# Two unused fills that shift tile addresses in an expert-choice MoE block, so that both matmul operands start at the same offset modulo 512 bytes

## The chip, the cores and the metric

One Trainium2 chip, one of its cores. The kernel is one program, launched once. The metric is the device time of one execution in microseconds (us); three executions of the kernel before took 1856.73 to 1860.6 us, with a median of 1858.37 us. Another execution was profiled, and all rows below come from it.

## The reference

One transformer block on a sequence of 1024 tokens of width 1024, in float32. What matters here is its second half, a mixture of 16 experts, and the projection ahead of it:

```python
mix = jnp.concatenate([y_mlstm, y_attn], axis=-1) @ w_out[l]
x = x + gate1 * mix
h2 = rms_norm(x, norm2_g[l]) * (1.0 + scale2) + shift2
...
cap = (EC_CAPACITY_FACTOR * S) // N_EXPERTS          # 128 tokens for each expert
gates, idx = lax.top_k(affinity.transpose(0, 2, 1), cap)
xin = h[bidx, idx]
hid = jax.nn.silu(jnp.einsum('becd,edf->becf', xin, w_gate)) * jnp.einsum('becd,edf->becf', xin, w_up)
y = jnp.einsum('becf,efd->becd', hid, w_down) * gates[..., None].astype(h.dtype)
```

Each expert takes 128 tokens through `w_gate` and `w_up` (1024 x 2048) and `w_down` (2048 x 1024). Ahead of that stand the input projection, an mLSTM mixer and a dilated attention.

## The kernel before

**Precision.** Float32 products are made of three products of a shorter type: each operand is split in a high part (rounded to `F32R`) and a low part (the rest), and hi x hi, lo x hi and hi x lo are added up in PSUM. In the names, `wh`/`wl`, `xTh`/`xTl`, `hTh`/`hTl`, `ogh`/`ogl` are such pairs; `hT` of the experts holds both parts in one tile.

**Experts (`phase_experts`).** The weights come in 384 pieces of 1 MB (128 partitions x 2048 floats), 24 for each expert, through a ring of ten buffers and some tiles that are reused for the same purpose. `feed` issues the load of a piece on SP's queue as soon as its buffer is free. `cut` splits a piece: ScalarE copies it into `wh` (line 1489), VectorE subtracts to get `wl` (line 1490). Both have three buffers. `mm` (line 1509) then runs 12 matmuls of 128x128 by 128x512 on it. The weight piece is the moving operand, 512 columns at a time; the stationary operand is a 128x128 slice of the transposed tokens `xTh`, `xTl` (gate and up) or of the transposed hidden values `hT` (down). For gate and up the order is four matmuls with `wh` and `xTh`, four with `wh` and `xTl`, four with `wl` and `xTh`; for down eight with `wh` and `hT` (high and low) and four with `wl` and `hT`. Each matmul has its own weight load (PEld), which runs beside the matmul before it.

So there are 16 x 16 x 12 = 3072 matmuls of the gate and up kind and 16 x 8 x 12 = 1536 of the down kind. Between them TensorE makes small transposes (of `xin`, line 1523, and of `hid`, line 1545, six groups for each expert) and eight small matmuls that pick the next expert's tokens (line 1436).

**Output projection (`mix_stream`, `phase_out`).** Here `ogh`, `ogl`, `mix` and `yal` are stationary and `wmh`, `wml`, `woh`, `wol` moving (lines 1069 to 1071 and 1174 to 1176; 384 matmuls of 512 columns).

**Earlier stages.** In `phase_start`, `gates_proj` and `gate_stream` (lines 337, 339, 341) and in `proj_stream` (lines 398 to 400) the operands are `hTh`/`hTl` and split pieces of `w_in`, also with 512 columns.

**Where tiles lie.** Tiles are given out from pools. Pools lie one behind the other from the low end of a partition, or with `side="right"` from its high end, and what is added in an early pool shifts all later pools of its side. The pool `consts` (`k.cp`, opened first on the low side) holds tiles of 512, 512, 32, 32, 512, 256 and 128 bytes for each partition and starts at address 16512, so what follows on that side (`og`, `ya`, and in their buffers `xTl`, `hT`, `ogl`, `yal`) starts at 64 modulo 512. Byte offsets modulo 512 of the operands, in the built programs:

| stage | stationary | moving | before: stationary / moving | after |
|---|---|---|---|---|
| start and projection (L337-341, L398-400) | `hTh`, `hTl` or split `w_in` | the other | 448 / 448 | 448 / 448 |
| experts, gate and up | `xTh` | `wh`, `wl` | 0 / 0 | 0 / 0 |
| experts, gate and up | `xTl` | `wh` | 64 / 0 | 0 / 0 |
| experts, down | `hT` | `wh`, `wl` | 64 / 0 | 0 / 0 |
| output projection | `ogh`, `mix` | `wm*`, `wo*` | 192 / 192 | 0 / 0 |
| output projection | `ogl`, `yal`, three tiles of four | `wmh`, `woh` | 64 / 192 | 0 / 0 |
| output projection | `ogl`, `yal`, one tile of four | `wmh`, `woh` | 192 / 192 | 0 / 0 |

`xTh`, `wh` and `wl` lie at the high side (addresses from 159232 up), `xTl` and `hT` at the low side (from 18496 and from 34880).

Of the kernel before, what the change touches and what calls it, by code (L numbers as in the profile page):

```python
# [11 lines left out]
F32 = mybir.dt.float32  # L12
# [8 lines left out]
P = 128  # L21
# [77 lines left out]
def interleave(*streams):  # L99

    live = [[0.0, n, g, w] for n, (g, w) in enumerate(streams)]
    while live:
        s = min(live, key=lambda x: (x[0], x[1]))
        try:
            s[0] += next(s[2]) * s[3]
        except StopIteration:
            live.remove(s)


class K:  # L110
# [3 lines left out]
    def pool(self, name, stack, bufs=1, space=None, side=None):  # L114
# [4 lines left out]
            kw["side"] = side  # L119
        return stack.enter_context(self.tc.tile_pool(**kw))  # L120

    def split(self, hi, lo, src):
        self.nc.scalar.activation(hi, src, AF.Copy)  # L123
        self.nc.vector.tensor_sub(lo, src, hi)  # L124
# [16 lines left out]
    def consts(self):  # L141
        nc, I = self.nc, self.I
        cp = self.cp
        self.ident = cp.tile([P, P], F32, name="ident")
        make_identity(nc, self.ident)
        self.ones = cp.tile([P, P], F32, name="ones")
        nc.vector.memset(self.ones, 1.0)
        self.c_sb = cp.tile([P, KT], F32, name="c_sb")
        nc.scalar.dma_start(out=self.c_sb, in_=I["c"].rearrange("o (p k) -> p (o k)", k=KT))
        self.sc = cp.tile([P, KT], F32, name="silu_c")  # L150
        self.w4 = self.tmp.tile([P, 3, MH, 4], F32, name="w4")
        for q, name in enumerate(("w_q_blk", "w_k_blk", "w_v_blk")):
            src = I[name]
            nc.gpsimd.dma_start(out=self.w4[:, q], in_=bass.AP(tensor=src.tensor, offset=src.offset, ap=[[4, P], [4 * P, MH], [1, 4]]))

        self.vec_rows = {}
        self.vcols = cp.tile([P, P], F32, name="vcols")
        self.amat = self.mc.tile([P, MH, P], F32, name="amat")
        self.bdv = self.mc.tile([P, MH, P], F32, name="bdv")
        self.mask = self.mc.tile([P, 2, P], F32, name="mask")  # L160
        self.gbias = self.mc.tile([36, 2], F32, name="gbias")
        self.gqk = cp.tile([P, AE], F32, name="gqk")
        self.modc = cp.tile([P, 4 * KT], F32, name="mod_cols")
        rows = self.tmp.tile([P, P], F32, name="vrows")
        nc.vector.memset(rows, 0.0)
        at = 0
        for name, n in (("b_ada", 48), ("norm1_g", 8), ("conv_w", 20), ("conv_b", 4), ("mlstm_norm_g", 4), ("mlstm_skip", 4), ("norm2_g", 8)):
            src = I[name]
            nc.gpsimd.dma_start(out=rows[at:at + n, :], in_=bass.AP(tensor=src.tensor, offset=src.offset, ap=[[P, n], [1, P]]))
            self.vec_rows[name] = at  # L170
            at += n
        self.vrows = rows
# [12 lines left out]
    def phase_start(self):  # L185
# [6 lines left out]
        with ExitStack() as st:  # L192
# [50 lines left out]
            w_next()  # L243
            consts = self.mlstm_consts()
            next(consts)
            mods = []

# [22 lines left out]
            def modulate(k):  # L270
# [3 lines left out]
                self.split(self.hTh[:, k, :], self.hTl[:, k, :], xT[:, k, :])  # L274

            side = itertools.chain(consts, self.attn_tables())
            ada_half(0)
            ada_load(1, own())
# [865 lines left out]
    def phase_out(self):  # L1144
# [4 lines left out]
        with ExitStack() as st:  # L1149
# [55 lines left out]
            for k in range(MH):  # L1205
                if k == MH - 1:
                    for _ in merge:
                        pass
                prep(k)
                if k == 1:  # L1210
                    for i in range(NT):
                        x_load(i)
                for n in range(2 * G1):
                    mm(pss[n], n // 2, n % 2, k)
                    next(consts, 1)
                    if n % 2:
                        next(merge, 1)
# [406 lines left out]
def body(tc, I, out):  # L1624
    with ExitStack() as ctx:
        k = K(ctx, tc, I, out)
        st_ps = ExitStack()
        k.psA = k.pool("ps_a", st_ps, bufs=4, space=PSUM)
        k.psB = k.pool("ps_b", st_ps, bufs=4, space=PSUM)
        k.cp = k.pool("consts", ctx)  # L1630
        k.st_tmp, k.st_proj, k.st_y, k.st_mp = ExitStack(), ExitStack(), ExitStack(), ExitStack()
        k.mc = k.pool("mlstm_const", k.st_proj, side="right")
        k.tmp = k.pool("tmp", k.st_tmp)
        k.consts()
        k.phase_start()
        k.gates_proj()
        k.qkv_d = tc.dram_tile([3, S, ML], F32, name="qkv_d")
        st_cw = ExitStack()
        k.cw = k.pool("mlstm_work", st_cw, side="right")
        k.tags = dict(W=2, qw=2, kw=2, q=1, v=2, h=1, xc=2)  # L1640
        interleave((k.proj_stream(), 1.0), (k.mlstm_stream(), 1.9), (k.ada_stream(), 1.0))
        st_cw.close()
        k.st_mp.close()
        k.yap = k.pool("ya", k.st_y)
        k.ya = [k.yap.tile([P, S], F32, name="ya", bufs=MH) for i in range(MH)]
        st_r, st_aa = ExitStack(), ExitStack()
        k.aa = k.pool("attn_in", st_aa)
        k.pairs, k.kl = {}, {}
        k.ta = k.pool("attn_t", st_aa)
        k.attn_load_qk(0)  # L1650
        k.attn_load_1(0)
        for n, _ in enumerate(k.gate_stream()):
            if n == PAIR0[0]:
                k.attn_pair_norm(0)
                T = k.attn_pair_T(0, lambda: k.psB.tile([P, 512], F32, name="pb"), k.ta)
            if n == PAIR0[1]:
                k.attn_load_2(0)
            if n >= PAIR0[2]:
                next(T, 0)
        for _ in T:  # L1660
            pass
        k.st_proj.close()
        st_ps.close()
        st_m = ExitStack()
        k.m1 = k.pool("moe1", st_m, side="right")
        k.rp = k.pool("rows", st_r, side="right")
        k.mx = k.pool("mix", st_r, side="right")
        st_at = ExitStack()
        k.phase_attn(st_at)
        st_at.close()  # L1670
        st_aa.close()
        st_rt = ExitStack()
        k.rt = k.pool("route", st_rt)
        st_ps = ExitStack()
        k.psm = k.pool("ps_m", st_ps, bufs=8, space=PSUM)
        st_w = ExitStack()
        k.ring = [k.pool("ring_a", st_w, bufs=EARLY)]
        k.flow, k.fed, k.ready = k.pieces(), [], []
        k.phase_out()
        st_r.close()  # L1680
        k.m2 = k.pool("moe2", st_m, side="right")
        k.ring.append(k.pool("ring_b", st_w, bufs=RING - EARLY))
        k.route_select()
        st_ps.close()
        st_ps = ExitStack()
        k.psx = k.pool("ps_x", st_ps, bufs=4, space=PSUM)
        k.psy = k.pool("ps_y", st_ps, bufs=4, space=PSUM)
        k.phase_experts()
        st_ps.close()
        st_w.close()  # L1690
        st_rt.close()
        k.st_y.close()
        st_m.close()
# [29 lines left out]
```

## Time and profile before

| | |
|---|---|
| median of three runs | 1858.37 us (1856.73 to 1860.6) |
| the profiled execution's own time | 1857.18 us |
| its span, from the first to the last instruction | 1855.5 us |
| mean granted TensorE clock | 0.983 of full speed |
| TensorE (PE) busy | 1738.8 us, 94% |
| VectorE (DVE) busy | 1486.8 us, 80% |
| ScalarE (ACT) busy | 1206.2 us, 65% |
| GpSimd (POOL) busy | 179.6 us, 10% |
| bytes moved by DMA | 517.39 MB, mean 279 GB/s |

The experts take the span from about 720 us on. "Busy" of an engine is the union of its instructions' times. A matmul's own duration contains its run through the array, so matmuls overlap in the records; how fast they follow each other is read from the starts, as the time from one start to the next (the pace).

### The profile page before, as it was taken

How to read it: one execution, taken by the hardware profiler on the slowest of the kernel's cores; microseconds unless marked ns; L12 is line 12 of the kernel's file. 1: busy time of each engine (PE TensorE's matmuls, PEld its weight loads, DVE VectorE, ACT ScalarE, POOL GpSimd, SP SyncE). 2: the span in 40 equal slices, each digit the busy share in tenths (PEclk: the TensorE clock that was granted, in tenths of full speed). 3: DMA queues.
4: the chain of work that ended last, by engine and by line, in shares of the span. 5: the costliest groups of instructions: out<-in, count | busy, mean ns of one | idle time of the engine just before them, and what ended most of it. 6: DMA issues, size and time to landing. Idle time of an engine off the chain costs nothing. (4 is left out here: it accounts for less than half of the span.)

```text
span 1855.5 us, 24345 instructions
## 1 busy us (share of the span) xinstructions
PE 1738.8 (94%) x8685; PEld 1400.1 (75%) x8685; DVE 1486.8 (80%) x2147; ACT 1206.2 (65%) x1596; POOL 179.6 (10%) x176
## 2 busy tenths in 40 slices
PE   5999999999998939999999999999999999999997
PEld 4777788778886727888888777787777777777875
DVE  5578885687865778988988888898888888988976
ACT  5346454477763438777777677777776776777764
POOL 1001000031122010011011000100100001000001
PEclk9999999999999959999999999999999999999999
DMA  8135662435648777999999999999999999999991
GB/s 321 47 108 188 208 209 89 108 89 118 139 112 239 270 306 278 382 356 371 392 351 389 348 347 351 362 367 358 352 343 383 349 354 360 336 377 356 357 357 23
DMA packets 150536, 517.39 MB, mean 279 GB/s; under 512 B 32938, under 2 KB 50736, under 8 KB 112784
## 3 DMA queue, kind: packets, MB, share of 16 engines
q1 hardware_dynamic: 136832, 482.07, 70.6%
q0 software_dynamic: 10528, 33.18, 7.1%
q8 instruction: 68, 1.11, 0.2%
q10 hardware_dynamic: 3056, 0.61, 0.2%
q14 instruction: 52, 0.43, 0.1%
HBM read 488.29 MB, written 27.50 MB: 278 GB/s over the span
## 5 line engine op out<-in xcount | busy, mean ns | idle before, releaser
L1490 DVE TENSOR_TENSOR wl<-w,wh 128x2048 fp32r<-128x2048 f32 x295 | 663.2, 2279 | 72.9 <-ACT wh L1489 72.0
L1489 ACT ACTIVATE wh<-w 128x2048 fp32r<-128x2048 f32 x295 | 557.7, 1914 | 120.2 <-PE px L1509 56.3
L1490 DVE TENSOR_TENSOR wl<-w_half,wh 128x1024 fp32r<-128x1024 f32 x178 | 207.9, 1218 | 8.3 <-ACT wh L1489 8.2
L1489 ACT ACTIVATE wh<-w_half 128x1024 fp32r<-128x1024 f32 x178 | 179.8, 1059 | 36.8 <-PE px L1509 16.3
L1509 PE MATMUL px<-wl,xTh 128*128 128x512 f32 x512 | 142.5, 398 | 10.0 <-DVE wl L1490 10.0
L1509 PE MATMUL py<-wl,xTh 128*128 128x512 f32 x512 | 142.6, 398 | 8.9 <-DVE wl L1490 8.8
L1509 PE MATMUL px<-wh,xTh 128*128 128x512 f32 x512 | 141.9, 397 | 3.5 <-ACT wh L1489 1.9
L1509 PE MATMUL py<-wh,xTh 128*128 128x512 f32 x512 | 142.6, 396 | 0.8 <-ACT wh L1489 0.7
L1509 PE MATMUL px<-wh,xTl 128*128 128x512 f32 x512 | 141.4, 397 | 0.0
L1509 PE MATMUL py<-wh,xTl 128*128 128x512 f32 x512 | 141.1, 395 | 0.0
L1509 PE MATMUL px<-wh,hT 128*128 128x512 f32 x512 | 131.5, 397 | 0.0
L1509 PE MATMUL py<-wh,hT 128*128 128x512 f32 x512 | 130.8, 397 | 0.2 <-ACT wh L1489 0.2
L1509 PEld LDWEIGHTS px<-wl,xTh 128*128 128x128 f32 x512 | 94.8, 189 | 38.7 <-DVE wl L1490 18.1
L1509 PEld LDWEIGHTS py<-wl,xTh 128*128 128x128 f32 x512 | 94.1, 188 | 38.1 <-DVE wl L1490 17.8
L1562 POOL DMA_INDIRECT out_dram<-xin,idx x16 | 52.6, 3288 | 661.2 <-DVE xin L1561 661.2
L1509 PEld LDWEIGHTS px<-wh,xTh 128*128 128x128 f32 x512 | 95.2, 189 | 26.6 <-ACT wh L1489 3.6
L1509 PEld LDWEIGHTS px<-wh,xTl 128*128 128x128 f32 x512 | 96.8, 189 | 21.9
L1509 PEld LDWEIGHTS py<-wh,hT 128*128 128x128 f32 x512 | 95.1, 188 | 23.4 <-ACT wh L1489 0.9
L1509 PEld LDWEIGHTS py<-wh,xTh 128*128 128x128 f32 x512 | 94.4, 188 | 24.2 <-ACT wh L1489 3.1
L1509 PEld LDWEIGHTS py<-wh,xTl 128*128 128x128 f32 x512 | 96.1, 188 | 21.8 <-DVE xTl L124 0.2
L1509 PEld LDWEIGHTS px<-wh,hT 128*128 128x128 f32 x512 | 95.0, 188 | 22.6 <-ACT wh L1489 0.4
L398 PE MATMUL pa<-wh,hTh 128*128 128x512 f32 x192 | 78.9, 412 | 1.6 <-ACT wh L355 1.5
(452 smaller groups left out, 3091.9 us busy)
## 6 DMA issues: line engine op xcount, KB each, us to landing
w<-in_w_gate_dram SPq DMA_DIRECT2D x99, 1024.0 KB, 7.3
w<-in_w_down_dram SPq DMA_DIRECT2D x99, 1024.0 KB, 9.6
w<-in_w_up_dram SPq DMA_DIRECT2D x94, 1024.0 KB, 6.2
w_half<-in_w_up_dram SPq DMA_DIRECT2D x62, 512.0 KB, 7.2
w_half<-in_w_gate_dram SPq DMA_DIRECT2D x56, 512.0 KB, 8.2
w_half<-in_w_down_dram SPq DMA_DIRECT2D x56, 512.0 KB, 8.7
ada_w<-in_w_ada_dram SPq DMA_DIRECT2D x64, 256.0 KB, 3.4
wraw<-in_w_in_dram SPq DMA_DIRECT2D x20, 512.0 KB, 4.5
```

The source lines that it names most:

```text
L398: nc.tensor.matmul(ps, hTh[:, k, t], hi[k], start=(k == 0), stop=False)
L1489: self.nc.scalar.activation(h[:, c], t, AF.Copy)
L1490: self.tc.keep_in_program_order(self.nc.vector.tensor_sub(l[:, c], t, h[:, c]))
L1509: nc.tensor.matmul(ps[c], x[:, t], y[:, o:o + 512], start=first and q == 0 and t == 0, stop=last and (q, t) == (2, FF // N - 1))
L1562: nc.gpsimd.indirect_dma_start(out=self.out, out_offset=bass.IndirectOffsetOnAxis(ap=u["idx"][:, :1], axis=0), in_=y, in_offset=None, comp ...
```

## The change

A helper `fill` allocates a tile that nobody reads, and writes zeros to it on GpSimd. It is called twice: 448 bytes per partition in `consts`, ahead of all other tiles of that pool, and 192 bytes in `rows`, on the high side, ahead of the pools of the output projection. The first shifts everything behind it on the low side up by 448 bytes, the second the pools behind `rows` down by 192 bytes. `consts` is opened for the whole kernel; `rows` is closed before the experts begin.

```diff
@@ -119,6 +119,10 @@
             kw["side"] = side
         return stack.enter_context(self.tc.tile_pool(**kw))
 
+    def fill(self, pool, n):
+
+        self.nc.gpsimd.memset(pool.tile([P, n // 4], F32, name="fill"), 0.0)
+
@@ -141,6 +145,7 @@
         cp = self.cp
+        self.fill(cp, 448)
         self.ident = cp.tile([P, P], F32, name="ident")
@@ -1664,6 +1669,7 @@
         k.rp = k.pool("rows", st_r, side="right")
+        k.fill(k.rp, 192)
         k.mx = k.pool("mix", st_r, side="right")
```

Of the instructions' order it moves little: two writes are added on GpSimd, and one pair of instructions on VectorE changes places. Lines of the changed kernel are 4 to 6 higher. GpSimd's queue at the start of the program, before:

```order
L1715 MEMSET const-uint8-127 128x1
L1719 UNCONDITIONAL_BRANCH
masks.py:197 MEMSET ident 128x128
L154 DMA w_80<-in_w_q_blk_dram 128x4x4
masks.py:199 ISA
```

and now:

```order
L1721 MEMSET const-uint8-127 128x1
L1725 UNCONDITIONAL_BRANCH
L124 MEMSET fill 128x112
masks.py:197 MEMSET ident 128x128
L159 DMA w_82<-in_w_q_blk_dram 128x4x4
masks.py:199 ISA
```

The fill stands ahead of `ident` and of the first small loads. The second fill stands in the same queue in the attention, ahead of two writes to `kTl` (lines 770 before, 775 now), which before follow the products `qk` directly. Now:

```order
L763 TENSOR_TENSOR qk<-qk,gqk 128x1024 x2
L124 MEMSET fill 128x48
L775 MEMSET kTl_3708 64x1024
L775 MEMSET kTl_3710 64x1024
L1059 TENSOR_TENSOR wo_raw<-wo_raw,gate_3433 128x512 x2
```

VectorE's queue in the normalization at the start (`n_v` and `n_y` belong to the second half of `x`, `vcols` are constants that a transpose on TensorE delivers), before:

```order
L453 TENSOR_TENSOR bdv<-bmask,w_80 128x128 x4
L133 TENSOR_SCALAR n_v<-ss_111 128x4
L134 TENSOR_SCALAR n_y<-n_v 128x4
L178 COPY vcols<-pa 128x128
L136 TENSOR_TENSOR n_t<-n_y 128x4
```

and now:

```order
L458 TENSOR_TENSOR bdv<-bmask,w_82 128x128 x4
L137 TENSOR_SCALAR n_v<-ss_113 128x4
L183 COPY vcols<-pa 128x128
L138 TENSOR_SCALAR n_y<-n_v 128x4
L140 TENSOR_TENSOR n_t<-n_y 128x4
```

The copy of `vcols` goes ahead of `n_y`. On TensorE, ScalarE and SP's queue the instructions and their order are the same.

## Rows read from the trace of the kernel before

**Rows 1.** Windows of the experts: length, busy us by engine, clock, DMA share, GB/s.

```profile
760.00:1000.00 240.00, 240.00 (x1101) 195.00 (x1100) 214.56 (x158) 182.79 (x161) 26.23 (x7) 1.00 0.97 375
1000.00:1800.00 800.00, 777.44 (x3486) 616.12 (x3485) 681.51 (x492) 577.40 (x516) 52.89 (x21) 1.00 0.95 357
```

**Rows 2.** Waits of TensorE from 720 us on: total us, times, longest.

```profile
PE px L1509 <- DVE wl L1490: 11.5, 19, 1.4
PE py L1509 <- DVE wl L1490: 9.0, 15, 1.4
```

**Rows 3.** Timeline of TensorE in the start stage: start us, length, instruction, count.

```profile
97.38 0.62 PE L341 MATMUL pa<-hTh,wg_l 128*128 128x512 f32 x2
...
102.82 0.62 PE L341 MATMUL pa<-hTh,wg_l 128*128 128x512 f32 x2
```

**Rows 4.** Timeline of TensorE in a gate product of the experts.

```profile
1197.88 1.08 PE L1509 MATMUL px<-wh,xTh 128*128 128x512 f32 x4
...
1203.43 0.85 PE L1509 MATMUL px<-wh,xTh 128*128 128x512 f32 x3
```

**Rows 5.** Windows as in rows 1, around rows 3 and rows 4.

```profile
97.40:103.80 6.40, 6.40 (x30) 5.31 (x29) 0.00 (x0) 0.00 (x0) 0.00 (x0) 1.00 0.30 80
1195.00:1209.00 14.00, 13.59 (x59) 10.56 (x58) 11.58 (x7) 9.17 (x6) 1.45 (x1) 1.00 0.99 370
```

**Rows 6.** Timeline of TensorE in narrow windows, inside two groups of rows 4.

```profile
1201.12 0.61 PE L1509 MATMUL px<-wh,xTh 128*128 128x512 f32 x2
1201.57 0.40 PE L1509 MATMUL px<-wh,xTl 128*128 128x512 f32 x1
1202.04 0.63 PE L1509 MATMUL px<-wh,xTl 128*128 128x512 f32 x2
```

**Rows 7.** Timeline of TensorE in a down product, up to the next transposes.

```profile
1136.13 1.56 PE L1509 MATMUL px<-wh,hT 128*128 128x512 f32 x6
1137.53 1.09 PE L1509 MATMUL px<-wl,hT 128*128 128x512 f32 x4
1138.46 1.03 PE L1523 MATMUL py<-ident,xin 128*128 128x128 f32 x8
```

**Rows 8.** Timeline of TensorE in the projection, after smaller matmuls; one row each.

```profile
306.50 0.39 PE L399 MATMUL pa<-wl,hTh 128*128 128x512 f32 x1
...
308.11 0.39 PE L400 MATMUL pa<-wh,hTl 128*128 128x512 f32 x1
...
308.79 0.40 PE L400 MATMUL pa<-wh,hTl 128*128 128x512 f32 x1
```

**Rows 9.** A wait of TensorE in the experts: timeline of TensorE and VectorE.

```profile
1046.34 0.35 PE L1436 MATMUL py<-route_rhs,oh 128*128 128x5 bf16 x8
...
1047.20 4.49 DVE L1490 TENSOR_TENSOR wl<-w,wh 128x2048 fp32r<-128x2048 f32 x2
...
1049.55 0.73 PE L1509 MATMUL px<-wl,xTh 128*128 128x512 f32 x2 [1.36 <-DVE wl L1490]
```

**Rows 10.** Waits of SP's queue and landing of loads, 1000 to 1800 us.

```profile
SPq L1472 <- DVE wl L1490: 445.0, 203, 6.1
w<-in_w_down_dram SPq DMA_DIRECT2D x72, 1024.0 KB, 9.3
```

**Rows 11.** Timeline of GpSimd and VectorE at the start; of GpSimd and `kTl` in the attention.

```profile
0.81 0.21 POOL masks.py:197 MEMSET ident<- 128x128 f32 x1 [0.29 <-POOLq L1715]
18.00 0.17 DVE L134 TENSOR_SCALAR n_y<-n_v 128x4 int32<-128x4 int32 x1
381.85 1.95 POOL L770 MEMSET kTl<- 64x1024 f32 x2
L790 DVE TENSOR_TENSOR kTl<-tp,kTh x12: 673/689/696, 404.8 to 505.1; 64x512 fp32r<-64x512 f32 x12
```

**Rows 12.** The page's groups: busy us and mean ns of one, idle before.

```profile
L1509 PE MATMUL px<-wl,xTh 128*128 128x512 f32 x512 | 142.5, 398 | 10.0 <-DVE wl L1490 10.0
L1509 PE MATMUL px<-wh,xTl 128*128 128x512 f32 x512 | 141.4, 397 | 0.0
```

## The prediction

> **What bounds the kernel now.** I read the windows of the experts first, because they take the span from 720 us on. Between 760 and 1000 us TensorE is busy in all 240.00 us, and from 1000 to 1800 us in 777.44 of 800 us, at full clock (1.00, so 2.4 GHz) [rows 1]. VectorE is busy in 89% and 85% of these stretches, ScalarE in 76% and 72%. The waits of TensorE come next: 34 waits for the low part of a weight piece, 20.5 us in all, none longer than 1.4 us [rows 2]. So TensorE sets the time, and the question is how fast its matmuls follow each other.
>
> That I read from starts in the timeline. In the start stage, from 97.38 to 102.82 us, twelve rows of two matmuls each pass: 24 matmuls of 512 columns in 5.44 us, 226.7 ns each [rows 3]. In a gate product, from 1197.88 to 1203.43 us, six rows of four pass: 24 matmuls of the same shape in 5.55 us, 231.3 ns each [rows 4]. The clock is 1.00 in both [rows 5]. 226.7 ns is the fastest steady pace that I find for this shape. In the start stage all operands have equal offsets modulo 512 bytes; in the experts `xTl` differs by 64 from the weights.
>
> Inside a group it shows finer. The last two matmuls on `xTh` (equal offsets) before the change to `xTl` take 1201.57 - 1201.12 = 0.45 us; the first two on `xTl` take 1202.04 - 1201.57 = 0.47 us [rows 6]. VectorE, ScalarE and the DMAs are busy throughout [rows 5], so the slower pace comes with the operand, not with the traffic. In the down product, where every stationary operand is off by 64, ten matmuls take 1138.46 - 1136.13 = 2.33 us, 233 ns each [rows 7].
>
> **The change, part by part.** It makes all these offsets equal, moves no work on TensorE, and adds two small writes.
>
> *Gate and up.* 3072 matmuls from 231.3 to 226.7 ns: 3072 x 4.6 ns = 14.1 us less.
>
> *Down.* 1536 matmuls from 233 to 226.7 ns: 1536 x 6.3 ns = 9.7 us less. Together 23.8 us, if all of them reached the steady pace at once.
>
> *Settling.* They don't. After smaller matmuls the projection, with equal offsets, needs some time: the seven matmuls from 306.50 to 308.11 us take 230 ns each, and only the next three (0.68 us) 226.7 [rows 8]. That is 7 x 3.3 ns = 0.02 us for one restart. In each expert the run of matmuls is cut by six groups of transposes, one routing group and two or three waits, about 10 times, so 160 times in all. I take 0.03 us each, since other restarts are slower than this one: 4.8 us back. The matmul right at the cut is governed by the cut, not by the pace; 160 x 5 ns = 0.8 us more. 23.8 - 5.6 = 18.2 us.
>
> *What waits give back.* Where TensorE waits for VectorE, the end of the wait is set by a chain that doesn't get faster. In the example, VectorE waits for the routing matmuls, then starts the low part at 1047.20 us, and TensorE resumes at 1049.55 us: 3.2 us from 1046.34 on, whatever the pace of the matmuls between [rows 9]. With 34 such waits [rows 2] that is 109 us of some 1070 us of expert matmuls. I round it up to an eighth, because a few waits have a longer lead-in: 2.3 us of the 18.2 are given back as longer waits for `wl`.
>
> *Output projection.* 384 matmuls; the 96 on the shifted parts of `ogl` and `yal`, and those that settle behind them, gain at most 384 x 4.6 ns = 1.8 us. Many runs there are short, so I take 0.5 us.
>
> *Fills.* The write of `ident`, which is larger than either fill, takes 0.21 us [rows 11]. The first fill delays `ident` and the first small loads by up to that; TensorE needs `ident` for the first time only after `x` has been scaled, so it is hidden. Without that cover it costs 0.2 us. The second fill stands before the write to `kTl` at 381.85 us; VectorE first fills that tile at 404.8 us [rows 11], so 20 us cover it. On VectorE, `n_y` now stands behind the copy of `vcols`, which waits for TensorE; the scaling behind it comes 0.17 us later [rows 11], and I count 0.2 us.
>
> *Loads.* TensorE needs pieces about 2% faster. SP's queue waits 445 us of 800 for VectorE to free a buffer, not for a transfer, and a piece lands 9.3 us (median, the slowest kind) after its issue [rows 10], while a ring of ten buffers lasts 12 x 231.3 ns x 10 = 27.8 us. Between 760 and 1000 us the loads kept up at 375 GB/s, against 357 GB/s later [rows 1]; 2% on top of 357 is 364. Nothing to pay. If the loads could not exceed 375 GB/s, only the unbroken stretches would lose part of their gain, some 4 us.
>
> *Sum.* 18.2 - 2.3 + 0.5 - 0.2 = 16.2 us. Against the profiled execution's own 1857.2 us that is 1841.0 us; the median of the runs is 1.2 us higher, which gives 1842.2, so I say **1842 us**. Ends of the terms: without settling and give-back 24 us (1834 us); with half of the gain given back, 8 us (1850 us).
>
> One rule of the Trainium skill speaks against all of this. The page "SBUF — State Buffer", section "Who interferes with whom", says that TensorE has two independent read ports, one for the moving operand and one for weight loads, and never waits on anyone; by that, two addresses cannot matter and the gain would be zero. The trace disagrees so far: at the same clock and shape the pace is 226.7 ns in one place and 231 to 233 in others [rows 3, 4, 7].
>
> **Rivals.**
>
> *The side of the memory, not the offset (0.11).* Everything that runs slower has its stationary operand at the low end of a partition (`xTl`, `hT`) and its moving operand at the high end; everything at 226.7 ns has both at the high end. The change moves `xTl` and `hT` by 448 bytes only, so they stay where they are. Then nothing changes on TensorE, and the time is 1858.4 + 0.2, about 1858.5 us. For it: no row separates the two readings. Against it: distance alone has no reason to cost a few nanoseconds, a pattern of offsets has.
>
> *The pace depends on no address (0.03).* Then something else in the experts' stage makes the 4.6 ns, and again nothing changes: about 1858.5 us. The two ends of rows 6 lie within one microsecond of each other and differ, which speaks against it. This is the case of the page named above.
>
> *All is given back (0.06).* VectorE is busy in 85 to 89% [rows 1] and works in a fixed order; if each of the 34 waits grew by half a microsecond, 17 us would be gone. Time 1850 to 1858 us. Against it: between 760 and 1000 us TensorE never waits, with VectorE at 89%.
>
> *Slower: equal offsets collide (0.08).* Two reads that begin at the same offset at the same time might disturb each other. The groups of the page allow it: 512 matmuls on `wl` and `xTh` (equal offsets) take 142.5 us, 512 on `wh` and `xTl` (unequal) 141.4 [rows 12], 2.1 ns more for each. The change puts 2560 more matmuls on equal offsets; at 2.1 ns that is 5.5 us, so 1858.4 + 5.5 = 1864 us. It decides from 1.5 ns on (2560 x 1.5 ns = 3.7 us, 0.2%). Against it: `wl` and `xTh` follow `xTl`, so they may still be settling, and a start stage with nothing but equal offsets is the fastest of all [rows 3].
>
> **How the numbers follow.** 0.72 for the forecast, the rest as given. Its own range is 1834 to 1850 us. Two readings of no change hold 0.14, so the range goes on to 1858.8 us; the slower rival is left out, with a tenth of the forecast's own. A measurement of this kernel can tell about 0.2%, 3.7 us, from no change. Faster by more: the forecast and half of the give-back case, 0.75. Within it: 0.17. Slower: 0.08.
>
> **What would show it.** In the profile after, `hT` and `xTl` runs should come at 227 ns: 24 gate matmuls in 5.44 us instead of 5.55, ten down matmuls in 2.27 instead of 2.33. The waits for `wl` should grow by some 2 us in all, with VectorE's and ScalarE's durations unchanged. If the pace stays at 231 to 233 ns, the offset was not the cause. If it falls to 227 and the time doesn't move, the give-back was underrated. If the matmuls on `xTh` become slower as well, equal offsets collide.

## The result, and the profile after

| | before | after |
|---|---|---|
| median | 1857.57 us (4 runs, 1856.73 to 1860.6) | 1843.86 us (4 runs, 1842.88 to 1845.79) |
| ratio | | 0.9922, 95% interval 0.9908 to 0.9936 |
| the profiled execution, and its span | 1857.18, 1855.5 us | 1843.23, 1841.5 us |

The change saves 13.7 us between the medians; 16.2 were forecast, and 1842 us. In the traces all of it comes from the experts: the first matmul of an expert starts at the same time in both (682.75 us before, 682.86 after), and the rest of the span is 14 us shorter. In the kernel before:

```profile
682.75 1.65 PE L1509 MATMUL px<-wh,xTh 128*128 128x512 f32 x3 [1.61 <-ACT xTh L123]
```

The timeline of TensorE after, with that row, a wait (with VectorE's rows, like [rows 9]), a down product (like [rows 7]) and a gate product (like [rows 4]); columns are start in us, length, engine, line, instruction, count, and idle time before with what ended it:

```profile
682.86 2.07 PE L1514 MATMUL px<-wh,xTh 128*128 128x512 f32 x4 [1.61 <-ACT xTh L127]
...
1040.52 0.35 PE L1441 MATMUL py<-route_rhs,oh 128*128 128x5 bf16 x8
...
1041.39 4.49 DVE L1495 TENSOR_TENSOR wl<-w,wh 128x2048 fp32r<-128x2048 f32 x2
...
1043.73 1.20 PE L1514 MATMUL px<-wl,xTh 128*128 128x512 f32 x4 [1.36 <-DVE wl L1495]
...
1129.36 1.52 PE L1514 MATMUL px<-wh,hT 128*128 128x512 f32 x6
1130.71 1.07 PE L1514 MATMUL px<-wl,hT 128*128 128x512 f32 x4
1131.63 1.03 PE L1528 MATMUL py<-ident,xin 128*128 128x128 f32 x8
...
1196.18 1.07 PE L1514 MATMUL px<-wh,xTh 128*128 128x512 f32 x4
...
1201.62 1.98 PE L1514 MATMUL py<-wh,hT 128*128 128x512 f32 x8
```

24 gate matmuls now take 1201.62 - 1196.18 = 5.44 us, 226.7 ns each, where [rows 4] has 5.55; ten down matmuls take 1131.63 - 1129.36 = 2.27 us, where [rows 7] has 2.33. Those are the two numbers that the prediction named. The wait is what it was: from the routing matmuls to the resumption 1043.73 - 1040.52 = 3.2 us, and TensorE is idle for 1.36 us, both as in [rows 9].

The windows of the experts after (the second ends 14 us earlier than in [rows 1], as the stage does); the x behind TensorE's busy time counts its matmuls, the small ones and transposes too:

```profile
760.00:1000.00 240.00, 240.00 (x1119) 198.19 (x1116) 217.16 (x160) 186.38 (x167) 26.23 (x7) 1.00 0.98 381
1000.00:1786.00 786.00, 762.06 (x3458) 610.47 (x3458) 676.50 (x490) 572.14 (x509) 52.88 (x21) 1.00 0.96 361
```

In the 240 us without idle time TensorE gets through 1119 matmuls instead of 1101, 1.6% more. That one number shows the change best, because TensorE's busy share is the same 240.00 us in both. The loads follow: 381 and 361 GB/s instead of 375 and 357.

The page's groups after, like [rows 12], and the waits of TensorE from 720 us on, like [rows 2]:

```profile
L1514 PE MATMUL px<-wl,xTh 128*128 128x512 f32 x512 | 140.6, 395 | 10.3 <-DVE wl L1495 10.3
...
L1514 PE MATMUL px<-wh,xTl 128*128 128x512 f32 x512 | 138.5, 391 | 0.0
```

```profile
PE px L1514 <- DVE wl L1495: 12.0, 19, 1.4
PE py L1514 <- DVE wl L1495: 9.6, 16, 1.4
```

Even the group with `wl` and `xTh`, whose offsets were equal before, is 1.9 us faster; why is seen below. The waits for `wl` are 21.6 us instead of 20.5: 1.1 more, where the prediction named some 2.

### The profile page after: what moved, and what is told of

Its sections match the earlier page's. It is cut to its first block, busy times and chain, and to the rows that moved or that the text cites. A ratio compares the mean times of both kernels' runs of the same rounds, so it can differ in the third digit from the quotient of the medians.

```text
span 1841.5 us, 24346 instructions
## 1 busy us (share of the span) xinstructions
PE 1726.5 (94%) x8685; PEld 1402.6 (76%) x8685; DVE 1486.4 (81%) x2147; ACT 1206.0 (65%) x1596; POOL 178.3 (10%) x178
```

## The experiments

From each trace I take three numbers besides the time. The *stage* is the span less the start of the first expert matmul; it leaves out the part ahead of the experts, which varies by itself (in the two traces of the changed kernel they start at 682.9 and 685.2 us). The *pace* is the distance between the starts of successive expert matmuls of 512 columns, for those that follow at least 13 of their kind without a break. The *excess* is the sum of (distance - 226.7 ns) over all expert matmuls that another one follows within 245 ns, some 4250 of 4608. Ratios are to the kernel before on the same chip; the medians of different rows can come from different chips (the kernel before took 1857.57 to 1859.49 us on them).

| kernel | experts' offsets, stationary / moving | median us | ratio, 95% interval | stage us | pace ns | excess us |
|---|---|---|---|---|---|---|
| before | 0 and 64 / 0 | 1857.57 | | 1172.7 | 231.6 | 22.2 |
| after | 0 / 0 | 1843.86 | 0.9922 (0.9908 to 0.9936) | 1158.7 | 226.7 | 5.7 |
| after, again | 0 / 0 | 1846.22 | 0.9933 (0.9920 to 0.9947) | 1159.3 | 226.8 | 6.0 |
| weights moved | 0 / 448 | 1864.23 | 1.0024 (1.0015 to 1.0034) | 1177.4 | 233.3 | 28.2 |
| first fill only | 0 / 0 | 1845.11 | 0.9915 (0.9897 to 0.9934) | 1159.0 | 226.7 | 5.5 |
| second fill only | 0 and 64 / 0 | 1860.17 | 1.0012 (0.9998 to 1.0025) | 1173.2 | 231.6 | 22.3 |
| low side at 256 | 0 and 256 / 0 | 1845.63 | 0.9916 (0.9899 to 0.9934) | 1159.9 | 226.7 | 5.7 |
| low side at 192 | 0 and 192 / 0 | 1850.59 | 0.9957 (0.9941 to 0.9974) | 1164.9 | 229.0 | 11.9 |
| identity at 0 | 0 / 0 | 1847.18 | 0.9935 (0.9922 to 0.9947) | 1158.9 | 226.8 | 5.8 |
| routing on GpSimd | 0 / 0 | 1850.11 | 0.9949 (0.9934 to 0.9965) | 1155.8 | 226.7 | 5.8 |
| routing on ScalarE | 0 / 0 | 1841.31 | 0.9904 (0.9887 to 0.9920) | 1151.8 | 226.7 | 6.2 |

The theory was the prediction's: the distance between the offsets of the two operands (that of the stationary operand less that of the moving one) sets the pace. The rivals were the side of the memory, no address at all, and equal offsets that collide.

**1. The pace by itself, at many distances.** A small program with operands at both ends of the memory; while its series run, no other engine works and DMA moves at most 1 GB/s:

```diff
+        for o in OFFS:
+            run(f"lh{o}b", "lowst", "highmv", (o,))
+        for st, mv, c in (("lowst", "lowmv", "ll"), ("highst", "highmv", "hh"), ("highst", "lowmv", "hl")):
+            for o in (0, 64, 256):
+                run(f"{c}{o}b", st, mv, (o,))
...
+        run("mix4b", "lowst", "highmv", (0, 0, 0, 0, 64, 64, 64, 64))
```

> This kernel computes nothing of the block: it copies x to the output, and beside that TensorE runs long series of 96 matmuls, 128x128 by 128x512, one series for each pair of offsets (the letters of a series say on which side of the partition the stationary and the moving operand lie, l low and h high; the number is the distance of their offsets in bytes; eq moves both together; mix4 has four matmuls at 0 and four at 64 in turn; each512 steps the stationary operand by 512). Offset theory: lh0, lh512, ll0, hh0, hl0, eq64, eq256, eq448 and each512 run at 226.7 ns from start to start, and every other distance at 231 to 234, wherever the operands lie. Side theory: ll and hh run at 226.7 at every distance, lh and hl at 231 or more at every distance, 0 included. If a smaller modulus does it, 256 (or 128, 64) runs at 226.7 as well.

Timeline of TensorE there. Each row is a series of 96 matmuls; its pace is the start of the next row less its own, over 96. The name gives the sides of the stationary and the moving operand (l low, h high) and the distance in bytes; in `eq448b` both operands stand at 448:

```profile
148.99 22.55 PE L41 MATMUL lh64b<-highmv,lowst 128*128 128x512 f32 x96
171.38 22.65 PE L41 MATMUL lh96b<-highmv,lowst 128*128 128x512 f32 x96
...
216.18 22.14 PE L41 MATMUL lh192b<-highmv,lowst 128*128 128x512 f32 x96
238.16 21.93 PE L41 MATMUL lh256b<-highmv,lowst 128*128 128x512 f32 x96
259.93 22.56 PE L41 MATMUL lh320b<-highmv,lowst 128*128 128x512 f32 x96
282.32 22.48 PE L41 MATMUL lh384b<-highmv,lowst 128*128 128x512 f32 x96
...
436.72 21.92 PE L41 MATMUL hh0b<-highmv,highst 128*128 128x512 f32 x96
458.48 22.56 PE L41 MATMUL hh64b<-highmv,highst 128*128 128x512 f32 x96
480.88 21.95 PE L41 MATMUL hh256b<-highmv,highst 128*128 128x512 f32 x96
...
612.19 21.93 PE L41 MATMUL eq448b<-highmv,lowst 128*128 128x512 f32 x96
633.96 22.41 PE L41 MATMUL mix4b<-highmv,lowst 128*128 128x512 f32 x96
656.20 21.95 PE L41 MATMUL each512b<-highmv,lowst 128*128 128x512 f32 x96
```

With both operands on one side, 0 bytes give 21.76 us / 96 = 226.7 ns and 64 bytes 22.40 / 96 = 233.3. With the operands on opposite sides, 64 bytes give 22.39 / 96 = 233.2. So the side does nothing, and no load or other engine is needed for the loss. With both operands moved to 448 the pace is 21.77 / 96 = 226.8: what counts is the distance, not either address. But a distance of 256 is as good as 0 (21.77 / 96 = 226.8) and 192 lies between (21.98 / 96 = 229.0); 320 is back at 233.2. The expectation with 256 in place of 512 holds but for 192 (and 448, which is the same modulo 256): the distance has a direction. Modulo 256, 192 has the stationary operand 64 bytes behind the moving one and costs 2.3 ns; 64 has it ahead and costs 6.5. Where four matmuls at 0 and four at 64 take turns, the pace is 22.24 / 96 = 231.7, close to the experts' 231.6. The mean of the two paces would be 230.0: one slow operand slows its neighbours on the fast one as well.

**2. The fast operand made slow.** In the changed kernel the weights are moved away, so that all 4608 expert matmuls, those on `xTh` too, have 64 bytes between their operands:

```diff
+        k.fill(k.m1, 64)
...
-        k.fill(k.rp, 192)
+        k.fill(k.rp, 128)
```

> As the changed kernel, but a third fill of 64 bytes behind the weights' pool (and 128 instead of 192 bytes in rows) puts wh and wl of the experts at 448 modulo 512; xTh, xTl and hT stay at 0, and no tile changes sides. Offset theory: now all 4608 expert matmuls have unequal offsets, those on xTh too, which were equal before the change; steady pace 231 to 234 ns everywhere, time 1862 to 1870 us, slower than before the change (1857.6). Side theory: nothing that matters has moved, 226.7 ns and 1844 us.

The window from 760 to 1000 us, where TensorE never waits:

```profile
760.00:1000.00 240.00, 240.00 (x1096) 193.99 (x1095) 214.84 (x158) 181.46 (x159) 26.23 (x7) 1.00 0.97 374
```

1096 matmuls, against 1101 before and 1119 after, a pace of 233.3 ns and a time 0.24% above the kernel before. No operand changed its side, and the kernel holds one more fill; the rival of the side falls, and so does the one in which equal offsets collide. A distance of 0 - 448 is 64 modulo 256, so here the moving operand was shifted, with the effect that shifting the stationary one has.

**3. One fill at a time.** The first fill alone, then the second alone:

```diff
-        k.fill(k.rp, 192)
```

> Only the first fill (448 bytes in consts), without the second. Offset theory: the experts as in the changed kernel, 226.7 ns; the output projection keeps unequal offsets for ogl and yal (0 against 192), which costs 0.3 to 1 us; time 1844 to 1845 us. If the second fill carried a larger part, the time would lie nearer to 1850.

```diff
-        self.fill(cp, 448)
```

> Only the second fill (192 bytes), which moves the weights of the output projection from 192 to 0 and leaves ogl, yal, xTl and hT at 64: the experts run as in the kernel before (231.6 ns steady, excess 22 us), so no difference to it that can be measured, 1857 to 1859 us. If the gain of the changed kernel came from the high side after all: about 1844.

The same window with the first fill only, then with the second only:

```profile
760.00:1000.00 240.00, 240.00 (x1119) 198.00 (x1118) 216.72 (x160) 186.68 (x167) 26.23 (x7) 1.00 0.98 381
```

```profile
760.00:1000.00 240.00, 240.00 (x1102) 195.00 (x1101) 216.52 (x159) 182.75 (x161) 26.23 (x7) 1.00 0.97 376
```

The first fill makes the whole gain (0.9915), the second none that can be measured (1.0012, its interval holds 1). In the output projection the excess is 1.05 us with the first fill alone and 0.65 with both: 0.4 us is what the second is worth by this count; no time can show it.

**4. Which modulus.** The first fill is 256 bytes larger, then 192:

```diff
-        self.fill(cp, 448)
+        self.fill(cp, 704)
```

> As the changed kernel, but the first fill is 704 bytes, so xTl and hT stand at 256 modulo 512 against 0 for the weights. Offset theory with modulus 512: 231 to 234 ns on xTl and hT again, time 1856 to 1859 us. If equality modulo 256 is enough: 226.7 ns and 1844 us. If a shift as such mattered, or the side: 1844 or 1857.6, with xTl and hT at one pace.

```diff
-        self.fill(cp, 448)
+        self.fill(cp, 640)
```

> The changed kernel with the first fill of 640 bytes: xTl and hT at 192 modulo 256 against weights at 0, a distance at which the series of matmuls ran at 228.9 ns. If the pace of the series holds in the kernel: 2560 matmuls that take 2.2 ns more than equal ones, 5.6 us, so about 1849 us, between the changed kernel (1844) and the kernel before (1858); steady pace 228.4 in the mean over all expert matmuls. If any unequal distance costs the same in the kernel: 1858. If the experts' loss needs exactly 64: 1844.

The window of the kernel with the low side at 256, then at 192:

```profile
760.00:1000.00 240.00, 240.00 (x1119) 197.97 (x1118) 217.35 (x160) 186.68 (x166) 26.22 (x7) 1.00 0.99 383
```

```profile
760.00:1000.00 240.00, 240.00 (x1112) 196.79 (x1111) 215.38 (x160) 185.37 (x163) 26.23 (x7) 1.00 0.98 378
```

With 256 bytes between the operands the kernel is as fast as the changed one: ratio 0.9916, pace 226.7, 1119 matmuls in the window. With 192 it lies between, as the series said: pace 229.0, and 11.9 - 5.7 = 6.2 us more excess, where 5.6 were expected. The pace of 228.4 that was named was too low, for the slow operand's neighbours again: `wl` on `xTh`, at equal offsets, comes at 229.6. So the pace of a small series carries over to the kernel within a microsecond, and the modulus that counts is 256 bytes, not 512.

**5. What makes the matmuls settle.** The transposes and other small matmuls between the runs leave 5.7 us of excess. In the changed kernel `ident` lies at 64; the first kernel puts it at 0 and keeps the offsets of the experts' and the projection's operands:

```diff
-        self.fill(cp, 448)
+        self.fill(cp, 384)
...
+        nc.gpsimd.memset(cp.tile([P, 16], F32, name="tail"), 0.0)
```

> The changed kernel with the first fill 64 bytes smaller and a tile of 64 bytes at the pool's end: the experts' and the projection's operands lie as in the changed kernel, the identity moves from 64 to 0 modulo 512. Theory 1 (offsets in the transposes disturb what follows): the settling of the experts, 5.7 us of excess over 226.7 ns, falls to 2 to 4 us, and the time to about 1841 us, 0.998 of the changed kernel. Theory 2 (the change of shape makes it settle): excess 5.7 us, 1844 us as before.

The second is again a small program: series with cuts of four transposes, with the identity at 0 (`ia`) or 64 (`ib`) and the transposed tile at 0, 64, 128 or 4 (`xa` to `xd`), then products of other widths:

```diff
+            for i in range(12):
+                for j in range(n):
+                    nc.tensor.matmul(acc[j % 3][:, :cols], T["lowst"][:, f:f + P], T["highmv"][:, :cols], start=True, stop=True)
+                for j in range(small if ident is not None else 0):
+                    nc.tensor.transpose(acc[3][:, j * P:(j + 1) * P], src[:, o + j * P:o + (j + 1) * P], ident)
```

> Twelve times (12 matmuls of 512 columns and 4 transposes of 128) in a series; it computes nothing of the block. The stationary and moving operands of the matmuls have equal offsets in every series but two, which have 64 bytes between them. Theory 1 (offsets modulo 256 of whatever is streamed and whatever is loaded set the pace, transposes included): with the identity at the offset of the transposed tile the matmuls behind the transposes come at 226.7 ns at once; with 64 or 128 bytes between them the first 5 to 8 matmuls take 230 to 236 ns each, so 20 to 40 ns more for each cut. Theory 2 (any change of shape makes the matmuls settle anew): the same 20 to 40 ns with every placement of the identity, and none without transposes. Of the products with 64 bytes between the operands both expect 233 ns throughout. Products of 256 and 128 columns: if the loss is a fixed time for each pair of load and matmul, 64 bytes cost some 6.7 ns there too; if it is a share of the columns streamed, 3.4 and 1.7 ns. The further distances in steps of 16 bytes: periodic in 256, 227 to 229 ns only near 192 to 256, 232 to 234 elsewhere.

Its timeline; of a series with cuts the first row is shown, so that its length is the start of the next less its own:

```profile
60.78 32.80 PE L56 MATMUL nocut<-highmv,lowst 128*128 128x512 f32 x144
93.42 2.88 PE L56 MATMUL iaxa<-highmv,lowst 128*128 128x512 f32 x12
...
131.71 3.00 PE L56 MATMUL ibxa<-highmv,lowst 128*128 128x512 f32 x12
...
170.11 3.00 PE L56 MATMUL ibxb<-highmv,lowst 128*128 128x512 f32 x12
...
208.50 3.02 PE L56 MATMUL ibxc<-highmv,lowst 128*128 128x512 f32 x12
...
247.06 3.02 PE L56 MATMUL iaxd<-highmv,lowst 128*128 128x512 f32 x12
...
285.32 3.04 PE L56 MATMUL unequal<-highmv,lowst 128*128 128x512 f32 x12
...
363.05 23.27 PE L56 MATMUL half0b<-highmv,lowst 128*128 128x256 f32 x192
386.16 22.78 PE L56 MATMUL half64b<-highmv,lowst 128*128 128x256 f32 x192
408.78 22.95 PE L56 MATMUL half128b<-highmv,lowst 128*128 128x256 f32 x192
...
785.30 21.94 PE L48 MATMUL lh240b<-highmv,lowst 128*128 128x512 f32 x96
```

Without cuts, 144 matmuls take 93.42 - 60.78 = 32.64 us, 226.7 ns each. With twelve cuts a series takes 38.3 us with both at 0 (131.71 - 93.42), 38.4, 38.4 and 38.6 with the identity at 64, 38.3 with the tile at 4. Between these lie at most 0.03 us for a cut. In all of them the eleven matmuls behind the first of a run take 25 to 51 ns more than at 226.7 each, 38 with both at 0 (the first itself takes some 314 ns to its successor). The placement changes the amount, but not by equality: the least, 25, is with the tile at 4. So theory 2 holds in the main: a change of shape makes the matmuls settle, with equal offsets too. The kernel says the same: with `ident` at 0 the excess is 5.8 us and the stage 1158.9, as before the move (time 1847.18 us, 0.9935 of the kernel before on its chip, with an interval that overlaps the changed kernel's). Two expectations of the small program failed: in steps of 16 bytes the pace is 227 to 229 ns only at 0, 192 and 240, with 230.0 at 176 and 233.3 at 208 and 224; and for narrower products no loss at 64 bytes showed, as the last section tells.

**6. The waits that are left.** [Rows 9] led the 1.36 us waits back to VectorE, which waits for the routing matmuls and starts the low part late. Two versions of the changed kernel take that wait off VectorE. The first copies the result on ScalarE and calculates on GpSimd:

```diff
-        nc.vector.tensor_copy(rg, ps[:, :5])
-        nc.vector.scalar_tensor_tensor(idx, rg[:, 0:1], float(P), rg[:, 1:2], op0=OP.mult, op1=OP.add)
-        nc.vector.tensor_reduce(rg[:, 0:1], rg[:, 2:5], axis=AX.X, op=OP.add)
+        nc.scalar.activation(rg, ps[:, :5], AF.Copy)
+        nc.gpsimd.tensor_scalar(rg[:, 0:1], rg[:, 0:1], float(P), None, op0=OP.mult)
...
```

> The changed kernel with the copy of the routing result on ScalarE and its small arithmetic on GpSimd, so that VectorE no longer waits for the routing matmuls. If the waits of 1 to 1.4 us for the low part of a piece come from VectorE being held up by that wait, about 15 of them go: 1844 less up to 15 us, and at least 5 us for a partial effect. If VectorE is late there anyway by the sum of its work: the waits stay or move, within 3 us of 1844. If ScalarE becomes late with the high part through the longer wait that it then has: 1850 or more.

Waits of TensorE there from 720 us on (total us, times, longest), then the costliest of GpSimd's small operations (busy us, mean ns, idle before):

```profile
PE px L1517 <- DVE wl L1498: 7.7, 16, 1.4
PE py L1531 <- DMA xin<-h_d,idx: 5.6, 2, 3.3
PE py L1517 <- DVE wl L1498: 5.5, 13, 1.0
```

```profile
L1445 POOL TENSOR_SCALAR rg<-rg 128x1 f32<-128x1 f32 x16 | 16.2, 1012 | 406.2 <-ACT rg L1444 406.2
```

The waits for `wl` fall from 21.6 to 13.2 us, so the chain was read rightly. But five such operations on GpSimd stand ahead of each gather, this one 1012 ns in the mean on 128 numbers, and TensorE now waits 5.6 us for gathered tokens. Even so the stage is 2.9 us shorter than the changed kernel's. Ahead of the first expert the routing stands in the open: from the first routing matmul to the first expert matmul 16.1 us pass instead of 9.2, and that 6.9 us outweighs the gain. A time of 1850 us had been named, but for a late ScalarE; this mechanism had not. That the kernel is slower than the changed one is read from the trace; the intervals of the two ratios overlap.

The second version keeps GpSimd out of it; these lines stand in place of the same three on VectorE:

```diff
+        nc.scalar.activation(rg[:, 1:2], ps[:, 1:2], AF.Copy)
+        nc.scalar.activation(idx, ps[:, 0:1], AF.Identity, bias=rg[:, 1:2], scale=float(P))
+        nc.scalar.activation(rg[:, 2:5], ps[:, 2:5], AF.Copy, accum_out=rg[:, 0:1])
```

> The changed kernel with the routing result read from PSUM by ScalarE alone, in three instructions (a copy of one column, the index as scale and bias, the sum of the gates by accumulation): no VectorE and no GpSimd between the routing matmuls and the gather. Theory 1 (in the run with the arithmetic on GpSimd the long waits for the low part went, and what took their place was the gather that GpSimd's slow small operations made late): six or seven waits of 1.36 us shrink to 0.2 us, the waits for the gathered tokens stay as in the changed kernel, so 6 to 8 us less, about 1837 us. Theory 2 (VectorE's order is then another, and the waits come back elsewhere): within 2 us of the changed kernel, 1842 to 1846. ScalarE, which now waits for the routing matmuls, could hand out the high part late: then waits for it of 1 us and more, and 1844 to 1850.

Beside it the changed kernel ran once more:

> The changed kernel itself, beside the version with the routing on ScalarE on the same chip: 1844 us, within 2 us, and the same pace of 226.7 ns in the experts.

It took 1846.22 us, 0.2 outside the two that were allowed, at the expected pace.

Waits of TensorE with the routing on ScalarE, and its timeline at the place of [rows 9]:

```profile
PE px L1514 <- DVE wl L1495: 7.2, 17, 1.0
PE py L1514 <- DVE wl L1495: 5.6, 14, 1.0
```

```profile
1047.37 2.28 DVE L1495 TENSOR_TENSOR wl<-w,wh 128x2048 fp32r<-128x2048 f32 x1
...
1047.86 0.35 PE L1441 MATMUL py<-route_rhs,oh 128*128 128x5 bf16 x8
...
1049.70 1.20 PE L1514 MATMUL px<-wl,xTh 128*128 128x512 f32 x4
```

VectorE now starts the low part 0.5 us before the routing matmuls instead of 0.9 us behind them, and TensorE goes on without a wait. The waits for `wl` are 12.8 us, no gathered tokens are waited for in the experts, and the stage is 1151.8 us, 7.5 shorter than that of the changed kernel beside it. The time is 1841.31 us (4 runs, up to 1843.01) against 1846.22 (6 runs, from 1844.88): 4.9 us less, between the 6 to 8 of theory 1 and the 2 of theory 2, and the lowest median of all. What is missing lies ahead of the first expert. Its gathered tokens, in the changed kernel beside it and then in this version:

```profile
681.66 1.97 PE L1528 MATMUL py<-ident,xin 128*128 128x128 f32 x8 [5.31 <-DMA xin<-h_d,idx]
```

```profile
685.89 1.97 PE L1528 MATMUL py<-ident,xin 128*128 128x128 f32 x8 [8.49 <-DMA xin<-h_d,idx]
```

From the first routing matmul to the first expert matmul 12.4 us pass here, against 9.2 in the changed kernel beside it and 9.0 to 9.5 in all nine traces with the routing on VectorE. So the version makes this gather some 3 us late. It is issued only 0.1 us later behind the routing matmuls, but its issue on GpSimd takes 2.23 us instead of 1.05, and it lands 7.7 us after its start instead of 4.6; VectorE's subtraction already runs when it is issued. Whether that is the reason, no run shows.

## Why the prediction was right, point by point

**Gate and up, down.** The paces were read rightly: over the whole kernel before, gate matmuls come 231.3 ns apart and down matmuls 233.2, and after the change the settled pace is 226.7. The term was a little too large all the same. It charged the gain to all 4608 matmuls, but only 4258 are followed by another within 245 ns. Of the other 350, 110 stand ahead of a transpose or a routing group, some 40 ahead of a wait, and some 200 are followed after a longer step, mostly of 300 to 345 ns and often just behind a cut. Those long steps gained nothing: step against step, 66.3 us before and 66.5 after. With the 4258, 23.8 x 4258 / 4608 = 22.0 us, and the measured excess was 22.2. For the matmuls at the cuts the prediction took off only 0.8 us.

**Settling.** 5.6 us were set, 5.7 measured, in part by luck: 4.8 of the 5.6 were for settling, 160 restarts at 0.03 us each, and there were 188 runs to settle. The 0.03 us was right. Net, 22.2 - 5.7 = 16.5 us instead of 18.2; that is the largest part of the miss.

**Give-back.** 2.3 us were set. Step against step (the order on TensorE is the same in both traces), the 4245 steps that are within 245 ns in both take 16.4 us less, and all other steps 2.2 us more. So the sum was right, but its make-up only in part: the waits make 1.5 of it, those for `wl` 1.1; the steps behind the small matmuls make 0.5 and the long steps 0.2. In the example the reason held, since 3.2 us pass from the routing matmuls to the resumption whatever the matmuls do, but nothing was given back there: the idle time is 1.36 us in both traces. The durations of VectorE's and ScalarE's split stayed, as was said (2.29 and 1.92 us for a whole piece).

**Output projection.** 0.5 set; its excess falls from 1.01 to 0.65 us. **Fills, loads.** 0.2 set for the changed order on VectorE. The experts start at 682.86 us instead of 682.75, so neither the gain of the projection nor this loss shows there; as that start differs by 2.4 us between two traces of the changed kernel, they could not. The loads exceed the 375 GB/s that a rival limit would have held.

The sum: in the steps of the experts 16.4 - 2.2 = 14.2 us, by the spans 14.0 (the start and the end of the stage come 0.1 us later each), by the medians 13.7; 16.2 were forecast.

**Rivals.** The side of the memory: series on one side and on two sides agree, and the changed kernel loses 18.7 us of stage when its weights are moved and every operand stays on its side; it is then 4.7 us behind the kernel before. The prediction's argument against it, that being far apart has no reason to cost a few nanoseconds, was no evidence; the series are. No address: but for the fills' own writes, only addresses differ between the kernels of experiments 2 to 4. The rule of the Trainium skill that the prediction weighed ("SBUF — State Buffer", section "Who interferes with whom") gives TensorE two independent read ports and has it never wait on anyone. What the prediction drew from it, that two addresses cannot matter, the series contradict, at 226.7 and 233.3 ns with no other engine at work. Equal offsets collide: they are the fastest. All given back: 2.2 of 16.4 us was. The row that spoke for a collision, `wl` on `xTh` no faster than `wh` on `xTl` [rows 12], was a neighbour's loss: the slow operand just before it. Made equal, both groups became faster.

One part of the argument was right by luck: it said 512. By experiment 4 any first fill that moves the low side from 64 to a multiple of 256 would have done; the change as made meets both readings.

## What to carry to other kernels

Where one instruction shape has two paces in a trace at the same clock, compare the addresses of its operands before looking for traffic; a fill of some hundred bytes was worth 14 us here, and offsets equal modulo 256 were enough. Count the instructions that have the pace, not all of the kind: those in front of a cut or a wait gain nothing. And before an engine is relieved of a wait, ask what the work costs where it goes: the same three lines cost more than they won on GpSimd (6.9 us against 2.9, by the trace), and on ScalarE made the kernel 4.9 us faster.

## What the runs showed of the hardware

With a weight load for each matmul of 512 columns, at a granted clock of 1.00, the pace is 226.7 ns at distances of 0, 240 (21.94 us for the series, against 21.93 at 256) and 256 bytes, 229.0 at 192 and 448, and 230.0 to 234.2 at the others tried. At 0, 64 and 256, where it was tried, the side of the operands makes no difference. For 256 columns the order turns round: 192 matmuls take 386.16 - 363.05 = 23.11 us at distance 0 and 408.78 - 386.16 = 22.62 at 64, so 120 and 118 ns. So "equal is best" is a finding for this shape, not a rule. At 128 columns the five distances tried take 111.4 to 111.7 ns. For both widths a loss at 64 bytes had been expected. Why a distance changes the pace, no run shows.
